# One decoder block on one core: output projection by pairs of tiles, merged gate broadcasts, dense queries as float32r passes, constants filled in another place

## Chip, core and metric

One core of one Trainium2 chip. The metric is device microseconds from start to end of one execution; lower is better. The kernel before was timed three times.

## What is computed

One layer of a hybrid decoder block on 512 tokens of width 1024 (float32), cut from the reference:

```python
def rmsnorm(x, w):
    return x * rsqrt(mean(x * x, -1) + eps) * w

h = rmsnorm(x, norm_mix_w)                      # 1. mixer
proj = h @ w_in                                  # gated-DeltaNet group (4 heads) | mLSTM group (4 heads)
go = gated_delta_rule(...)                       # chunkwise recurrences with per-token gates
mh = mlstm_chunkwise(...)
x = x + concatenate([go, mh], -1) @ w_out        # output projection

q = rmsnorm(x, norm_xa_w) @ xa_wq                # 2. cross-attention to 256 memory tokens
k, v = split(rmsnorm(mem, norm_mem_w) @ xa_wkv, 2)
x = x + (softmax(q k^T / 16) v) @ xa_wo

# 3. PEER: per token and head, top-16 of 2 x 128 product keys -> 16 of 16384 experts, then gather
sc = einsum('thpd,hpnd->thpn', rmsnorm(x, norm_ffn_w) @ peer_wq, sub_keys)
x = x + sum_k gate_k * gelu(u[expert_k] . h) * v[expert_k]
```

## The kernel before

The 512 tokens are four tiles of 128. A matmul that must keep float32's accuracy is done in one of two ways. **Split:** `weights` loads a 512 KB piece into a buffer `w` (a DMA on SP's queue, line 246), ACT copies it to float32r (`hi`, line 236, or line 251 into other buffers), DVE or POOL subtracts that from the raw piece (`low`: line 223 on DVE, line 221 on POOL; the list `low_on` says whose turn it is), and three matmul passes hi·hi, hi·lo, lo·hi follow (line 271 in `proj`, line 284 in `projT`). **Whole:** the piece is used as float32 (line 313 in `times`), with no copy. The activations are split in the same manner when they are transposed (`transposed`: PE line 209, ACT line 211, DVE line 212), or kept whole (`whole`: lines 293 and 294).

The mixer (0 to 445 us) projects head by head, and runs the two recurrences' chains under the projections; a string, `ORDER_MIX`, sets the order in which the program writes these steps, and the tile framework's scheduler then orders each engine's instructions. Each head takes from `gates` the rows `br` (three kinds: the GDN's cumulated decay, and two for mLSTM) and broadcasts them over the partitions with a matmul against a selector `sel`: one per token tile into a quarter of a PSUM bank for a GDN head (line 452, read by DVE lines 454 and 455 and ACT line 456), one of 256 columns per tile into a bank for an mLSTM head (line 564, read by DVE line 566 and ACT line 568). The pool of those banks (`psB`, name `acc`) has two buffers.

The mixer's output projection is `residual`, called with all four tiles and `wout`: `proj` goes over two blocks of 512 columns, over four 512 KB pieces each, and over the four tiles, so that a piece serves 24 matmuls. `residual`'s evacuation adds the result to `X` (DVE line 699). Buffers `w`, `wh` and `wl` are two each.

Then `ORDER_XA` gives the program's order, with tiles 0 and 1 as the pair G0 (experts gathered row by row) and tiles 2 and 3 as the dense pair G1: `n` is the norm of a pair (ACT line 197 squares, DVE lines 174 to 183 the reciprocal root, DVE line 199 scales by the row `wr`), `q` its queries (`q104` means G1's blocks 0 to 3, `q148` its blocks 4 to 7), `s` and `x` the attention, `o` its output projection, `i0` the norm and transposes of G0 for the expert layer, `f0` and following that layer's scores. G0's queries are split (line 284), G1's are whole (line 313). The row `wr` is loaded on SP's queue into a weight buffer `wh`. POOL fills `rows_` (constants of the routing) with 48 small memsets at lines 1148 to 1150, behind the mixer.

Of the kernel before, what the change touches and what calls it, by code (L numbers as in the profile page):

```python
# [16 lines left out]
P = 128  # L17
# [38 lines left out]
ORDER_XA = ("w2 n0 q008 n1 s0 x0 s1 x1 q104 o0 w1 i0 q148 f0 f1 r6 "  # L56
# [19 lines left out]
def _body(ctx, tc, A, out, dbg):  # L76
# [248 lines left out]
    def bank4():  # L325
        return psB.tile([P, 4, P], F32, name="acc")
# [36 lines left out]
    def gates(ph, wk, hs, tiles):  # L363
# [58 lines left out]
        for i in range(n):  # L422
# [8 lines left out]
        return {ti: dict(beta=beta[:, i], cum=cum[:, i], enm=enm[:, i], br=br[:, i], cj=cj[:, i], beg=beg[:, i])  # L431
                for i, ti in enumerate(tiles)}

    def gdn(wk, items, gs, qkv, mixed):
# [15 lines left out]
        bc = bank4()  # L450
        for i, (h, ti) in enumerate(items):
            PE.matmul(bc[:, i], sel[:, h], gs[ti]["br"][:, 0], start=True, stop=True)
# [102 lines left out]
    def mlstm(wk, items, gs, qk, va, mixed):  # L555
# [5 lines left out]
        ET, es = wt("ET", 2), wt("eg", 2)  # L561
        for i, (h, ti) in enumerate(items):
            bc = bank()
            PE.matmul(bc[:, :256], sel[:, h], gs[ti]["br"][:, 1:3].rearrange("p a b -> p (a b)"),
                      start=True, stop=True)
            V.scalar_tensor_tensor(ET[:, i], bc[:, 128:256], gs[ti]["cj"][:, h:h + 1], maskT,
                                   op0=OP.add, op1=OP.add)
            SC.activation(es[:, i], bc[:, 0:128], AF.Exp)
# [30 lines left out]
    def mixer(tiles, aside):  # L599
        nt = len(tiles)  # L600
        with tc.tile_pool(name="mxp", bufs=nt) as ph, tc.tile_pool(name="mxw", bufs=2) as wk:
# [89 lines left out]
            residual(tiles, hs, "wout")  # L691
# [11 lines left out]
    def xattn():  # L703
# [4 lines left out]
        wr = row(1, wpool, name="wh")  # L708
# [18 lines left out]
        def query(g, blocks):  # L727
            def ev(nb, ps):
                SC.activation(qT[:, nb, cols(g)], ps, AF.Copy)
            if "f" in part(g):  # L730
                projected(part(g)["f"], len(g), A["wq"], blocks, ev)
            else:
                projT(part(g), len(g), A["wq"], blocks, ev)
# [401 lines left out]
    t = late.tile([P, 2, DB, 2 * P], F32R, name="dh0")  # L1135
    dh.append({"h": t[:, 0], "l": t[:, 1]})
    t = late.tile([P, 4, D], F32, name="dh1")
    dh.append({"f": eight(t), "room": t})
# [8 lines left out]
    for a in range(K):  # L1147
        G.memset(rows_[:, 0, a], float(start[a]))
        G.memset(rows_[:, 1, a], float(start[a] - start[a - 1] if a else 0))
        G.memset(rows_[:, 2, a], float(a))  # L1150
# [46 lines left out]
    for what in ORDER_XA.split():  # L1197
# [3 lines left out]
        elif kind == "q":  # L1201
            n, x, y = (int(c) for c in what[1:])
            query(GS[n], range(x, y))
        elif kind == "s":
# [26 lines left out]
        elif kind == "f":  # L1231
            first.scores(n)
# [93 lines left out]
```

## Time and profile before

| | |
|---|---|
| median of 3 runs | 1864.69 us (1860.12 to 1868.1) |
| the profiled execution | 1863.43 us |
| its span, first to last instruction | 1861.5 us |
| PE busy in the span | 1682.0 us (90%) |
| DVE busy | 1248.2 us (67%) |
| POOL busy | 849.9 us (46%) |
| ACT busy | 393.9 us (21%) |
| DMA traffic | 514.81 MB |

Times are microseconds unless marked ns. PE is the matmul engine, PEld its weight loads, DVE the vector engine, ACT the scalar engine, POOL GpSimd, SP the queue on which most transfers are issued. A name such as `pj<-W,dh` is output from inputs, by the program's names; L271 is line 271. Idle time in brackets stands ahead of the instruction, with what ended it. Matmuls overlap: their pitch is read from the distance of two starts, not from one's duration.

### The profile page before, as it was taken

What the parts mean: (1) busy time and instruction counts of PE and PEld (TensorE: products, weight loads), DVE (VectorE), ACT (ScalarE), POOL (GpSimd) and SP (SyncE); (2) the same over time, 40 slices, a digit from 0 to 9 for tenths busy, and PEclk for the clock granted to TensorE, in tenths of its full rate; (3) what the DMA queues carried; (4) which work ended last, traced back from release to release, by engine and by line L of the source; (5) the groups of instructions that cost most, each with busy time, mean ns of one, the idle gap of its engine ahead of it and who ended that gap; (6) DMA issues with size and microseconds to landing.
All of it is one profiled execution on the core that took longest, in us unless ns stands there. A gap on an engine that the chain in (4) does not pass through costs nothing.

```text
span 1861.5 us, 21345 instructions
## 1 busy us (share of the span) xinstructions
PE 1682.0 (90%) x7444; PEld 1240.6 (67%) x7444; DVE 1248.2 (67%) x2767; ACT 393.9 (21%) x784; POOL 849.9 (46%) x686
## 2 busy tenths in 40 slices
PE   4999999999799986996998979993899999999993
PEld 3787777787698863885887746662666666664441
DVE  5656655473422598999998876557666566566668
ACT  5433442564243121111222210000000000000000
POOL 2121111323312044567344656666666666666663
PEclk9999999999899988998999979997999999999997
DMA  4111111234524477999799999999999999999996
GB/s 138 63 57 35 57 40 46 69 102 149 168 88 162 149 261 269 350 335 372 259 332 408 367 385 410 410 410 410 410 410 410 409 410 409 410 409 409 409 411 257
DMA packets 165355, 514.81 MB, mean 277 GB/s; under 512 B 15616, under 2 KB 44416, under 8 KB 163456
## 3 DMA queue, kind: packets, MB, share of 16 engines
q0 software_dynamic: 76608, 286.30, 39.3%
q1 hardware_dynamic: 59712, 212.48, 30.9%
q10 hardware_dynamic: 28928, 14.68, 2.7%
q8 instruction: 58, 0.95, 0.2%
q14 instruction: 49, 0.40, 0.1%
HBM read 494.52 MB, written 18.87 MB: 276 GB/s over the span
## 4 chain that ended last, share of the span: by engine, by line
DMA 38%; PE 33%; DVE 19%; issue 4%; POOL 3%; ACT 2%; SPq 0%; DVEq 0%; POOLq 0%; ACTq 0%
PE pj L313 7%; PE pj L271 7%; DMA row<-in_pv,ids 7%; PE pj L284 6%; DMA W<-in_pv,ids 6%; DMA Vm<-in_pv,ids 5%; PE acc L445 4%; DMA row<-in_pu,ids 3%; DMA wl<-in_pv,ids 3%; DMA W<-gates__132 3%; PE acc L945 2%; DMA gates__132<-W 2%; DVE W L1100 2%; DMA wl<-in_pu,ids 2%; DMA KT<-in_pv,ids 1%
## 5 line engine op out<-in xcount | busy, mean ns | idle before, releaser
L1000 PE MATMUL o<-ld,W 128*128 128x512 f32 x832 | 370.9, 596 | 4.6 <-DVE W L953 4.6
L313 PE MATMUL pa<-dh,ld 128*128 128x256 f32 x1296 | 295.5, 381 | 34.7 <-ACT dh L972 34.2
L313 PEld LDWEIGHTS pa<-dh,ld 128*128 128x128 f32 x1296 | 247.3, 191 | 103.1 <-issue 38.2
L1000 PEld LDWEIGHTS o<-ld,W 128*128 128x128 f32 x832 | 158.8, 191 | 175.7 <-issue 167.3
L221 POOL TENSOR_TENSOR wl<-w,wh 128x1024 fp32r<-128x1024 f32 x38 | 92.4, 2434 | 348.8 <-ACT wh L236 294.7
L313 PE MATMUL pj<-dh,w 128*128 128x256 f32 x704 | 161.3, 383 | 0.0
L313 PEld LDWEIGHTS pj<-dh,w 128*128 128x128 f32 x704 | 133.4, 193 | 17.8 <-ACT dh L294 0.3
L1073 POOL DMA_INDIRECT W<-in_pu,ids x73 | 95.4, 1307 | 91.0 <-DVE W L1100 52.2
L1111 DVE SCALAR_TENSOR_TENSOR dh<-row,act,dh 128x1024 f32<-128x1024 f32 x72 | 92.5, 1284 | 53.8 <-DMA row<-in_pv,ids 53.5
L1073 POOL DMA_INDIRECT row<-in_pu,ids x74 | 98.5, 1331 | 64.4 <-issue 17.8
L1073 POOL DMA_INDIRECT row<-in_pv,ids x74 | 99.9, 1351 | 47.2 <-issue 17.9
L313 PE MATMUL pj<-dh 128*128 128x256 f32 x496 | 113.2, 383 | 0.0
L284 PE MATMUL pj<-hT,wh 128*128 128x512 f32 x320 | 111.9, 421 | 0.0
L972 ACT ACTIVATE W<-pa 128x256 f32<-128x256 f32 x65 | 25.0, 384 | 407.2 <-PE pa L313 397.5
L271 PE MATMUL pj<-wh,hT 128*128 128x512 f32 x320 | 106.1, 404 | 0.4 <-ACT hT L211 0.4
L1100 DVE SCALAR_TENSOR_TENSOR row<-row,dh 128x1024 f32<-128x1024 f32 x74 | 88.3, 1223 | 22.4 <-DMA row<-in_pu,ids 22.1
L313 PEld LDWEIGHTS pj<-dh 128*128 128x128 f32 x496 | 94.5, 193 | 12.6
L1100 DVE SCALAR_TENSOR_TENSOR W<-W,dh 128x1024 f32<-128x1024 f32 x73 | 88.4, 1221 | 17.2 <-DMA W<-in_pu,ids 17.2
L236 ACT ACTIVATE wh<-w 128x1024 fp32r<-128x1024 f32 x56 | 59.3, 1059 | 124.2 <-PE pj L271 64.1
L1000 PE MATMUL o<-ld,dh 128*128 128x512 f32 x192 | 85.2, 592 | 0.0
L1073 POOL DMA_INDIRECT wl<-in_pu,ids x41 | 56.6, 1380 | 49.1 <-DVE tv L783 18.6
L1073 POOL DMA_INDIRECT wh<-in_pu,ids x40 | 54.2, 1354 | 49.9 <-DVE wh L1100 22.3
(431 smaller groups left out, 3106.5 us busy)
## 6 DMA issues: line engine op xcount, KB each, us to landing
ld<-in_pv SPq DMA_DIRECT2D x128, 512.0 KB, 6.8
ld<-in_pt SPq DMA_DIRECT2D x81, 512.0 KB, 6.9
gates__132<-W ACTq DMA_DIRECT2D x16, 896.0 KB, 13.9
W<-gates__132 POOLq DMA_DIRECT2D x14, 1024.0 KB, 17.1
w<-in_pt SPq DMA_DIRECT2D x24, 512.0 KB, 6.9
dh<-in_pt SPq DMA_DIRECT2D x23, 512.0 KB, 6.9
w<-in_win SPq DMA_DIRECT2D x20, 512.0 KB, 3.5
w<-in_pwq SPq DMA_DIRECT2D x16, 512.0 KB, 4.7
```

The source lines that it names most:

```text
L221: G.tensor_tensor(out, a, hi, op=OP.subtract)
L236: SC.activation(hi, wt, AF.Copy)
L271: PE.matmul(acc[i], a[:, d, i * P:(i + 1) * P], b[:, z], start=d == 0 and m == 0, stop=d == DB - 1 and m == len(pairs) - 1)
L284: PE.matmul(acc[:, :n * P], a[:, d], b[:, d], start=d == 0 and m == 0, stop=d == DB - 1 and m == 2)
L313: PE.matmul(ps, w[:, d], h[:, d], start=d == 0, stop=d == DB - 1)
L445: PE.matmul(ps[:, i], l[:, i], r[:, i], start=True, stop=True)
L945: PE.matmul(ps[:, k], oj[:, a, :, k], og[:, g, a, :, k], start=g == 0, stop=g == 1)
L972: SC.activation(place(e), ps, AF.Gelu)
L1000: PE.matmul(outs[DENSE[i]][z], place(e)[:, i * P:(i + 1) * P], v[:, z * 512:(z + 1) * 512], start=e == 0, stop=e == NKEY - 1)
L1073: G.indirect_dma_start(out=row, out_offset=None, in_=A[table], in_offset=bass.IndirectOffsetOnAxis(ap=ids[:, s:s + 1], axis=0))
L1100: V.scalar_tensor_tensor(row, row, 1.0, hn, op0=OP.mult, op1=OP.mult, accum_out=act[ti][:, s:s + 1])
L1111: V.scalar_tensor_tensor(hn, row, w, hn, op0=OP.mult, op1=OP.add)
```

## The change

- **Output projection:** `low_on` becomes DVE alone, and `residual` is called twice, for tiles 0 and 1 and then for tiles 2 and 3, each with the whole of `wout`.
- **Broadcasts:** a GDN head broadcasts its decay row for all four tiles with one matmul of 512 columns, and an mLSTM head its two rows with two of 512 columns into two banks; ACT's exponential of the second is one instruction for four tiles.
- **Dense queries:** `query` uses the split path for both pairs, so that `norm` and `mix` write G1's transposes split too; the buffer `dh1` becomes float32r and is opened again as float32 after `q148`. `q148` moves ahead of `i0`.
- **Row `wr`:** loaded on POOL's queue into the last sixth of a big buffer (`up[:, 5]`), not on SP's into `wh`.
- **Constants:** `rows_` is filled by the same 48 memsets just ahead of the first scores (`f0`).

```diff
-ORDER_XA = ("w2 n0 q008 n1 s0 x0 s1 x1 q104 o0 w1 i0 q148 f0 f1 r6 "
+ORDER_XA = ("w2 n0 q008 n1 s0 x0 s1 x1 q104 o0 w1 q148 i0 f0 f1 r6 "
...
         bc = bank4()
+        PE.matmul(bc[:, :n], sel[:, items[0][0]], gs["br"][:, :, 0], start=True, stop=True)
         for i, (h, ti) in enumerate(items):
-            PE.matmul(bc[:, i], sel[:, h], gs[ti]["br"][:, 0], start=True, stop=True)
...
+        bc = [bank4(), bank4()]
+        for x in (1, 0):
+            PE.matmul(bc[x][:, :n], sel[:, items[0][0]], gs["br"][:, :, 1 + x], start=True, stop=True)
         for i, (h, ti) in enumerate(items):
-            bc = bank()
-            PE.matmul(bc[:, :256], sel[:, h], gs[ti]["br"][:, 1:3].rearrange("p a b -> p (a b)"),
-                      start=True, stop=True)
-            V.scalar_tensor_tensor(ET[:, i], bc[:, 128:256], gs[ti]["cj"][:, h:h + 1], maskT,
-                                   op0=OP.add, op1=OP.add)
-            SC.activation(es[:, i], bc[:, 0:128], AF.Exp)
+            V.scalar_tensor_tensor(ET[:, i], bc[1][:, i], gs[ti]["cj"][:, h:h + 1], maskT, op0=OP.add, op1=OP.add)
+        SC.activation(es, bc[0][:, :n], AF.Exp)
...
-            residual(tiles, hs, "wout")
+            low_on[:] = [V]
+            for k in range(0, nt, 2):
+                residual(tiles[k:k + 2], {z: t[:, :, k * P:(k + 2) * P] for z, t in hs.items()}, "wout")
...
-        wr = row(1, wpool, name="wh")
+        wr = row_(1, up[:, 5], G)
...
-            if "f" in part(g):
-                projected(part(g)["f"], len(g), A["wq"], blocks, ev)
-            else:
-                projT(part(g), len(g), A["wq"], blocks, ev)
+            projT(part(g), len(g), A["wq"], blocks, ev)
...
-    t = late.tile([P, 2, DB, 2 * P], F32R, name="dh0")
-    dh.append({"h": t[:, 0], "l": t[:, 1]})
-    t = late.tile([P, 4, D], F32, name="dh1")
-    dh.append({"f": eight(t), "room": t})
+    for i in range(2):
+        t = late.tile([P, 2, DB, 2 * P], F32R, name=f"dh{i}")
+        dh.append({"h": t[:, 0], "l": t[:, 1]})
...
-    for a in range(K):
-        G.memset(rows_[:, 0, a], float(start[a]))
-        G.memset(rows_[:, 1, a], float(start[a] - start[a - 1] if a else 0))
-        G.memset(rows_[:, 2, a], float(a))
+
+    def row_numbers():
+        for a in range(K):
+            for x, val in enumerate((start[a], start[a] - start[a - 1] if a else 0, a)):
+                tc.keep_in_program_order(G.memset(rows_[:, x, a], float(val)))
...
             query(GS[n], range(x, y))
+            if n and y == DB:
+                t = late.tile([P, 4, D], F32, name="dh1")
+                dh[1] = {"f": eight(t), "room": t}
...
+            if not n:
+                row_numbers()
             first.scores(n)
```

ACT's order at the end of the output projection (`wh` the float32r copy of a piece of `wout`, the L197 rows the squares of the first pair's norm, L251 the copies of the first query weights; the brackets name the engines and queues waited for). Before:

```order
L236 ACTIVATE wh<-w 128x1024 [waits DMAHW4_49,PE_49,Pool_49]
L236 ACTIVATE wh<-w 128x1024 [waits DMAHW5_49,DVE_49,PE_49]
L197 ACTIVATE W_4106,nss<-x 128x1024 [waits DMAHW7_49,DVE_49,PE_49]
L197 ACTIVATE W_4106,nss<-x 128x1024 [waits DVE_49]
L251 ACTIVATE W_4105<-w 128x1024 [waits DMAHW6_49]
L251 ACTIVATE W_4105<-w 128x1024 [waits DMAHW7_49]
```

and now:

```order
L236 ACTIVATE wh<-w 128x1024 [waits DMAHW3_49,DVE_49,PE_49]
L236 ACTIVATE wh<-w 128x1024 [waits DMAHW4_49,DVE_49,PE_49]
L236 ACTIVATE wh<-w 128x1024 [waits DMAHW5_49,DVE_49,PE_49]
L197 ACTIVATE W_4066,nss<-x 128x1024 [waits PE_49]
L197 ACTIVATE W_4066,nss<-x 128x1024
L251 ACTIVATE W_4065<-w 128x1024 [waits DMAHW6_49]
L251 ACTIVATE W_4065<-w 128x1024 [waits DMAHW7_49]
```

The squares still stand behind the last copy of `wout` and still wait for PE; no copy waits for POOL any more.

DVE's order through the output projection to the start of the norm (L223 the lows, L212 the activations' lows, L699 or L700 the evacuations, L174 the norm's first step). Before:

```order
L223 TENSOR_TENSOR wl<-w,wh 128x1024 x2
L212 TENSOR_TENSOR hT<-tr,hT 128x4x128 x8
L223 TENSOR_TENSOR wl<-w,wh 128x1024
L699 TENSOR_TENSOR x<-pj,x 128x512 x4
L223 TENSOR_TENSOR wl<-w,wh 128x1024
L699 TENSOR_TENSOR x<-pj,x 128x512 x4
L174 TENSOR_SCALAR nv<-nss 128x1
```

and now, from the first evacuation on:

```order
L700 TENSOR_TENSOR x<-pj,x 128x512
L223 TENSOR_TENSOR wl<-w,wh 128x1024
L700 TENSOR_TENSOR x<-pj,x 128x512
L223 TENSOR_TENSOR wl<-w,wh 128x1024 x3
L700 TENSOR_TENSOR x<-pj,x 128x512
L223 TENSOR_TENSOR wl<-w,wh 128x1024
L700 TENSOR_TENSOR x<-pj,x 128x512
L223 TENSOR_TENSOR wl<-w,wh 128x1024 x3
L700 TENSOR_TENSOR x<-pj,x 128x512 x2
L174 TENSOR_SCALAR nv<-nss 128x1
```

All lows of `wout` are DVE's, between the evacuations of each pair; the norm's first step still follows the last evacuations.

PE's order from the attention's output projection (L271 with 512 columns, 96 matmuls) to the expert layer's scores (L313 from `dh_4764` before, from `dh_4916` now), with the dense pair's queries (L313 from `dh_4049` before, L284 now) and the first pair's transposes (L293). Before:

```order
L271 MATMUL pj<-W_4105,dh_4048 128x512 x96
L313 MATMUL pj<-dh_4049,w 128x256 x11
L293 MATMUL tr<-UI,dh_4764 128x128 x8
L313 MATMUL pj<-dh_4049,w 128x256 x2
L293 MATMUL tr<-UI,dh_4764 128x128 x8
L313 MATMUL pj<-dh_4049,w 128x256 x3
L313 MATMUL pj<-dh_4049,W_4106 128x256 x16
L313 MATMUL pj<-dh_4764,w 128x256 x16
```

and now:

```order
L284 MATMUL pj<-dh_4057,W_4065 128x256 x68
L271 MATMUL pj<-W_4065,dh_4056 128x512 x96
L284 MATMUL pj<-dh_4057,W_4065 128x256 x96
L293 MATMUL tr<-UI,dh_4916 128x128 x16
L313 MATMUL pj<-dh_4916,w 128x256 x16
```

The last four query blocks are 96 split matmuls in a row now, and all 16 transposes stand behind them, ahead of the scores.

## Rows read from the trace of the kernel before

**Rows 1.** The page: its part 4, the chain of work that ended last, by engine.
```profile
DMA 38%; PE 33%; DVE 19%; issue 4%; POOL 3%; ACT 2%; SPq 0%; DVEq 0%; POOLq 0%; ACTq 0%
```

**Rows 2.** Busy time of each engine by stage (windows of the span; a row has the window, its length, then PE, PEld, DVE, ACT and POOL busy with their instruction counts, the granted TensorE clock as a share of full speed, the DMA engines' busy share and GB/s).
```profile
36.00:424.00 388.00, 370.87 (x2122) 303.27 (x2121) 230.69 (x574) 173.38 (x337) 80.98 (x37) 0.97 0.19 60
...
445.50:493.40 47.90, 47.61 (x215) 38.15 (x216) 12.67 (x17) 11.40 (x15) 12.72 (x6) 1.00 0.44 153
493.40:508.60 15.20, 4.17 (x19) 3.19 (x17) 13.14 (x35) 7.85 (x12) 6.95 (x50) 0.60 0.68 216
...
532.30:566.10 33.80, 33.80 (x179) 28.45 (x178) 7.23 (x13) 17.52 (x42) 2.35 (x1) 1.00 0.26 79
...
588.20:604.80 16.60, 15.94 (x82) 13.65 (x81) 6.25 (x27) 5.51 (x11) 0.00 (x0) 1.00 0.45 159
...
655.00:1100.00 445.00, 384.87 (x1917) 317.81 (x1916) 411.64 (x1251) 95.58 (x198) 239.34 (x196) 0.93 0.92 333
1100.00:1830.00 730.00, 695.72 (x2237) 425.88 (x2235) 465.58 (x464) 30.04 (x79) 471.71 (x358) 0.98 1.02 409
```

**Rows 3.** Timeline of the end of the memory's value projection (`wv`), which works on two tiles with the same weight path: start, duration, engine, line, operation, and in brackets the engine's idle time before it and what ended that.
```profile
435.50 1.06 ACT L236 ACTIVATE wh<-w 128x1024 fp32r<-128x1024 f32 x1 [3.71 <-DMA w<-in_wv]
...
439.04 1.64 SPq L246 DMA_DIRECT2D w<-in_wout  x2
...
439.06 0.50 PE L271 MATMUL pj<-wl,x 128*128 128x512 f32 x1 [1.44 <-POOL wl L221]
439.09 1.23 DVE L223 TENSOR_TENSOR wl<-w,wh 128x1024 fp32r<-128x1024 f32 x1 [7.34 <-ACT wh L236]
...
442.73 1.06 ACT L236 ACTIVATE wh<-w 128x1024 fp32r<-128x1024 f32 x1 [3.67 <-DMA w<-in_wout]
```

**Rows 4.** DMA issues between 380 and 500 us (count, size of one, median us from issue to landing), and the last line of the view of line 246, which issues the split weights' loads, between 400 and 560 us.
```profile
w<-in_wout SPq DMA_DIRECT2D x8, 512.0 KB, 3.7
x<-in_x SPq DMA_DIRECT2D x1, 2048.0 KB, 7.6
...
DMA to landing us min/median/max: 3.4/3.6/7.0
```

**Rows 5.** Timeline of the output projection's last two matmuls.
```profile
493.18 0.40 PE L271 MATMUL pj<-wl,hT 128*128 128x512 f32 x1
...
493.41 0.40 PE L271 MATMUL pj<-wh,hT 128*128 128x512 f32 x1
```

**Rows 6.** Timeline from the output projection's end to the first query matmul.
```profile
497.06 2.35 POOL L221 TENSOR_TENSOR W<-w,W 128x1024 fp32r<-128x1024 f32 x1 [0.89 <-ACT W L251]
...
499.37 2.34 POOL L221 TENSOR_TENSOR W<-wl,W 128x1024 fp32r<-128x1024 f32 x1
...
499.46 3.33 DVE L199 SCALAR_TENSOR_TENSOR W<-x,nr,wh 128x1024 f32<-128x1024 f32 x1
...
502.89 1.94 PE L209 MATMUL tr<-UI,W 128*128 128x128 f32 x8 [9.08 <-issue]
...
505.36 1.28 DVE L199 SCALAR_TENSOR_TENSOR W<-x,nr,wh 128x1024 f32<-128x1024 f32 x1
...
508.56 12.62 PE L284 MATMUL pj<-dh,W 128*128 128x256 f32 x97
```

**Rows 7.** The norm row's load in the timeline; the DMA issues of that row's kind between 480 and 515 us (size, median us to landing); then, from the view of line 191 (all loads of rows in the kernel: duration of the issue in ns, first and last start), an issue on POOL and the times to landing.
```profile
488.39 0.42 SPq L191 DMA_DIRECT2D wh<-in_nrow  x1
...
wh<-in_nrow SPq DMA_DIRECT2D x2, 512.0 KB, 5.4
...
L191 POOL DMA_DIRECT2D Vm<-in_nrow x1: 555/555/555, 1707.4 to 1707.4; - x1
...
DMA to landing us min/median/max: 5.4/7.9/17.4
```

**Rows 8.** Timeline of the queries: two evacuations of split query blocks on ACT (six blocks lie between the two rows), then the end of the dense pair's queries with the first pair's transposes for the expert layer, on PE, to the first matmul of that layer's scores.
```profile
516.35 0.36 ACT L729 ACTIVATE W<-pj 128x256 f32<-128x256 f32 x1
...
532.61 0.39 ACT L729 ACTIVATE W<-pj 128x256 f32<-128x256 f32 x1 [2.50 <-PE pj L284]
...
588.17 4.91 PE L313 MATMUL pj<-dh,w 128*128 128x256 f32 x22
593.30 1.06 PE L293 MATMUL tr<-UI,dh 128*128 128x128 f32 x8 [0.23 <-DVE nt L181]
...
595.66 1.06 PE L293 MATMUL tr<-UI,dh 128*128 128x128 f32 x8 [0.43 <-DVE dh L199]
...
597.86 7.07 PE L313 MATMUL pj<-dh,W 128*128 128x256 f32 x32
604.77 1.46 PE L313 MATMUL pj<-dh,w 128*128 128x256 f32 x6
```

**Rows 9.** The gates' broadcasts of the last mLSTM head in the timeline (a row merges the two broadcasts of 256 columns; each matmul leaves two records), what PE waited for at the broadcasts up to 446 us (total, times, longest), and one window of 25 us.
```profile
410.27 1.13 PE L564 MATMUL acc<-br,sel 4*128 4x256 f32 x4
...
412.95 1.12 PE L564 MATMUL acc<-br,sel 4*128 4x256 f32 x4 [0.67 <-ACT eg L568]
...
PE acc L452 <- DVE EG L455: 1.2, 1, 1.2
...
PE acc L564 <- ACT eg L568: 0.7, 1, 0.7
...
125.00:150.00 25.00, 24.49 (x94) 18.61 (x93) 13.13 (x36) 10.62 (x18) 2.41 (x1) 0.80 0.19 64
```

More of the change, by code (lines that the diff above doesn't have):

```diff
@@ L430, in gates @@
         V.tensor_tensor(beg, beg, beta, op=OP.mult)
-        return {ti: dict(beta=beta[:, i], cum=cum[:, i], enm=enm[:, i], br=br[:, i], cj=cj[:, i], beg=beg[:, i])
-                for i, ti in enumerate(tiles)}
+        return {"br": br, **{ti: dict(beta=beta[:, i], cum=cum[:, i], enm=enm[:, i], cj=cj[:, i], beg=beg[:, i])
+                             for i, ti in enumerate(tiles)}}
     def gdn(wk, items, gs, qkv, mixed):
```

## The prediction

> **What bounds the kernel now.** I read the chain of waits first: DMA holds 38% of it, PE 33%, DVE 19% [rows 1]. No one engine bounds the whole, so the next view is the one by stages [rows 2]. From 1100 to 1830 us the DMA engines are busy all the time at 409 GB/s, from 655 to 1100 us DVE is busy for 411.64 of 445 us with DMA at 0.92: these are the gathers and the dense experts, and the change doesn't touch them. Ahead of them PE is full: 370.87 of 388 us in the mixer's main part, 47.61 of 47.9 us in the output projection, all of 33.8 us at the attention, 15.94 of 16.6 us at the last dense queries. One stage is different: from 493.4 to 508.6 us PE works for 4.17 us, and the granted clock is 0.60 in the mean, so in part at the lower of its two levels (1.2, not 2.4 GHz). That is the norm between the projection and the queries.
>
> From the first scores of the expert layer (604.77 us, [rows 8]) the instruction order of every engine is the same before and after the change. So the result is the shift of that one moment, carried to the end; nothing behind it has slack to swallow a few microseconds, as the DMA stage is full. I sum up the shift, part by part, against the profiled execution (1863.43 us, of which the span is 1861.5). It lies 1.3 us below the median of the three runs.
>
> **Output projection by pairs: +3.7 us.** The matmuls are the same 192, at a pitch of 0.23 us [rows 5]. But a piece of `wout` now serves 12 of them, 12 x 0.2325 = 2.79 us, and so is loaded twice: 16 loads, 16 ACT copies, 16 lows on DVE, where there were 8 each. Does the supply keep up? The value projection ahead of it has just that shape, two tiles and 12 matmuls a piece, and PE waited there [rows 3]: 1.44 us for a low on POOL, while ACT had been idle 3.71 and 3.67 us for the load. One buffer's round is the load, from the issue at 439.04 to the copy at 442.73, 3.7 us, plus the copy, 1.06, plus a low on DVE, 1.23 [rows 3], with some 0.06 of handing over: 6.07 us. With two buffers that is 3.03 us a piece against 2.79, so 0.24 x 16 = 3.9 us at most. A replay of the rounds by hand, with `x` (2 MB, 7.6 us, [rows 4]) ahead of the third load and a start that hides the first two pieces, moves the projection's end from 493.8 to 497.5. Lower bound 0: the transposes at the start spread the first four pieces, and every load might land in the minimum of 3.4 us [rows 4], which gives 2.88 us a piece. Upper bound +9.4: in the value projection two pieces took 442.73 - 435.50 = 7.23 us [rows 3], 3.6 a piece, which would be 0.82 x 16 = 13 us less what the start hides. I take 3.7, since POOL's 2.4 us lows, part of those 3.6, are gone.
>
> **The gap behind it: 0.** It would be the obvious gain of pairs that the first pair's norm lies under the second pair's matmuls. The order says otherwise: ACT's squares stand behind the 14 last copies and wait for PE, DVE's chain stands behind the last evacuations. What follows is as before: squares, chain, and then the place where POOL's lows (497.06 to 501.71 us) hold DVE [rows 6]: the scaling of the first tile takes 3.33 us, that of the second, without POOL, 1.28. Both lows of the query weights stay on POOL, so PE again gets its first transpose some 9 us after the end, and its first query some 14.8 us after it (508.56 - 493.8).
>
> The row `wr` is the other question there. Before it was issued at 488.39, ahead of the projection's end [rows 7]. Now POOL issues it, and the memory that it goes to is set free only with the last matmul. An issue on POOL takes 0.56 us, landing 5.4 at the least, 7.9 in the median, 17.4 at the most [rows 7]. It is needed when DVE comes free of POOL's lows, 501.71 - 493.8 = 7.9 us after the end [rows 6]. So it costs 0 at 0.56 + 5.4 = 6.0, 0.6 at the median and 10.1 at the worst. I take 0, as the two such loads of this stage have 5.4 for their median [rows 7].
>
> **Merged broadcasts: -3 us.** PE streams as many columns as before; 12 matmul issues and handovers a head fall away, and in the mLSTM heads 12 exponentials of ACT become fewer and longer ones. Where does that reach the path? In the last head the second pair of broadcasts started 412.95 - 410.27 = 2.7 us behind the first, as the banks had to be read by DVE and ACT [rows 9]. Behind it the chain runs over the head's norm on DVE to the low that frees the buffer for `wout` (439.04, [rows 3]), so nearly all of it counts. Of the earlier heads' waits little does: PE itself waited for a broadcast's readers only 1.2 and 0.7 us in the whole mixer [rows 9]. I take 2.7 plus a little of these: 3. Bounds: a loss of 2, since one matmul of 512 columns must now wait for a whole bank, and since lows and chains change places on DVE; a gain of 7, of the 388 - 370.87 = 17.1 us in which PE is idle in this stage [rows 2].
>
> **Dense queries split: -2.4 and -3.25 us.** A whole block of 256 tokens-by-columns takes 7.07 / 2 = 3.5 us (3.45 between evacuations); a split one takes (532.61 - 516.35) / 6 = 2.71 us, though it has three passes [rows 8]. For the four blocks in the attention's stage, where PE is full [rows 2], that is 4 x 0.74 = 2.9 us less; I take off 0.5 for ACT's copy (1.06) in front of the attention's own evacuations, so -2.4, with -3 and -1 as ends. The other four now stand before `i0`. From 588.17 to 604.77, 16.6 us, PE did four whole blocks, 16 transposes (two rows of 1.06 us) and 0.66 us of waiting [rows 8]. After: 4 x 2.71 = 10.84, and 16 transposes behind it with their evacuations, 2.5 us, 13.35 in all: -3.25. The norm of G0 is hidden by these blocks: before, both tiles' transposes were ready by 595.66, 7.5 us from the stage's start, and 10.84 us cover that. The lows and copies of eight more pieces lie beside PE's work on ACT (17.52 of 33.8 us busy) and DVE (7.23) [rows 2]; were that cover gone, PE would wait a low of POOL, 2.35 us, a piece.
>
> **Constants: 0.** POOL's 48 memsets end before the low at 497.06, which waited 0.89 us for ACT [rows 6]. At the new place POOL has no one waiting for it.
>
> **Sum:** 3.7 + 0 - 3 - 2.4 - 3.25 = -4.95 us, 1858.5 by the profiled execution and 1859 to 1860 by the median; I say 1859. A measurement of this kernel can tell about 0.5%, 9.3 us, from no change; so the limits are 1855.4 and 1874.
>
> **The rivals.**
> First, the mixer gains more. Between 125 and 150 us the granted clock is 0.80 [rows 9]: that is 10 us at the lower level, 5 us of full work. If the merged GDN broadcasts take away the wait that lies ahead of it, another 7 us go (5, and the 1.2 + 0.7 of waits): 1852. For it: the broadcast heads each GDN chain. Against: the long waits of PE there come from the chain itself, not from line 452.
> Second, the change does what pairs seem to offer, and the first norm hides under the second pair: then PE's 9.08 us of idle time go, 1850. The order speaks against it.
> Third, the slower side: the loads set the projection's pace. From 3.03 us a piece on each further tenth costs 1.6 us; at the value projection's 3.6 us the projection costs 13, not 3.7: 1868, over the median before, and 1871 or more where the broadcasts give nothing. For it: the trace had loads of up to 7.0 us [rows 4], and `x` lies among these. Against: POOL is out of the round.
> Fourth, the row lands late, and DVE waits up to 10.1 us for it, with PE behind: 1869. For it: it now starts with the gap. Against: 5.4 us in this stage.
> A rule of the Trainium skill speaks against this move of the row: in SBUF — State Buffer, section on the two separate sides, its warning on DVE blocking a DMA says that descriptors of a DMA from GpSimd's queue can't be written while DVE runs an operation in a two-port mode. No run here shows it; by that rule the issue would wait for what DVE then runs, the last evacuation or a 128x1 step, and the sum would be worse by under 1 us.
>
> **How the numbers follow.** Forecast 62%, own range 1852 to 1867; first rival 14%, second 5%, third 13%, fourth 6%. Faster than 1855.4: 8 of the forecast's 62, with 13 of the first rival and 5 of the second, 26%. Slower than 1874: 4 of the third and 1 of the fourth, 5%. The rest, 69%, is within 0.5%. The range 1849 to 1870 leaves out some 2 in 10: the ends of the first two rivals below, of the last two above.
>
> **What would show it.** In the profile after: 16 copies of `wout` on ACT at a spacing near 3.0 us, with PE waiting for DVE's lows, and an end of the projection less than 4 us later in its own stage; the gap again near 15 us, with DVE's scaling held by POOL; no wait for the row; the last mLSTM broadcasts less than 1 us apart; query blocks at 2.7 us; and the first scores at about 599.7 us instead of 604.77. I am wrong if that moment moves by a different amount, or if it moves so and the end doesn't follow.

## The result and the profile after

The changed kernel took 1853.3 us in the median (1851.97 to 1853.88, 4 runs) against 1865.51 for the kernel before (1860.12 to 1868.1, now 4 runs): a ratio of 0.9922, 95% interval 0.9895 to 0.9949 (the two medians alone stand at 0.9935). It is faster, by 0.7 to 0.8%. Medians here and below are of runs at the usual mean clock (0.95 to 0.96 granted); one of the ten runs of the kernel with four broadcasts in a row took 2454.67 us at 0.65 and is left out. The forecast was 1859 within 1849 to 1870; the time is in the range, and past the limit of 1855.4 for "faster by over 0.5%", which had 26%. The span of the profiled run went from 1861.5 to 1851.6 us, 9.9 less.

The stages by landmarks, starts read from the two timelines (the first matmul of the projection, its last matmul's end, the first query matmul, the first matmul of the scores):

| | before | after | shift | forecast |
|---|---|---|---|---|
| mixer, to the first projection matmul | 445.56 | 434.25 | -11.3 | -3 |
| output projection | 48.25 | 53.17 | +4.9 | +3.7 |
| gap, to the first query | 14.75 | 15.12 | +0.4 | 0 |
| queries and attention, to the first scores | 96.21 | 91.72 | -4.5 | -5.65 |
| from there to the end | 1256.7 | 1257.3 | +0.6 | 0 |
| sum | | | -9.9 | -4.95 |

So one term is far off, the mixer's, and the others are near. The chain and the stages of the changed kernel, beside [rows 1] and [rows 2]:

```profile
DMA 36%; PE 33%; DVE 17%; issue 8%; POOL 4%; ACT 2%; ACTq 1%; SPq 0%; DVEq 0%; POOLq 0%
```

```profile
0.00:434.20 434.20, 395.19 (x2225) 320.31 (x2226) 260.42 (x707) 196.21 (x366) 95.75 (x57) 0.98 0.23 72
434.20:487.30 53.10, 49.74 (x215) 36.87 (x213) 27.41 (x30) 19.80 (x23) 0.00 (x0) 1.00 0.60 198
487.30:502.50 15.20, 3.82 (x17) 3.14 (x16) 13.20 (x34) 7.85 (x12) 5.38 (x3) 0.63 0.77 275
...
524.40:558.00 33.60, 33.60 (x228) 30.41 (x227) 12.24 (x19) 20.15 (x46) 5.04 (x3) 1.00 0.32 99
...
580.10:594.30 14.20, 13.75 (x114) 13.19 (x112) 8.44 (x29) 7.28 (x14) 4.64 (x49) 1.00 0.71 240
```

The windows have the columns of [rows 2]. The mixer's window, which starts at 0 here, is 434.2 long and PE is busy for 395.19 of it. PE is idle for 39.0 us; in the kernel before, the same stretch of 445.5 us had 403.9 busy and 41.6 idle:

```profile
0.00:445.50 445.50, 403.85 (x2262) 326.79 (x2262) 262.26 (x705) 199.31 (x380) 98.52 (x58) 0.98 0.22 71
```

Most of the gain, 8.7 of 11.3 us, is thus busy time of PE, although PE streams the same columns. The projection is no longer full: 49.74 of 53.1 us, where it was 47.61 of 47.9. The gap is as before, and the queries' stages are shorter, with PE busy for 33.60 of 33.6 and 13.75 of 14.2 us.

The projection in the timeline, ACT's copies of `wout` first, then what ACT waited for in the stage (total, times, longest), beside [rows 3]:

```profile
445.24 1.06 ACT L236 ACTIVATE wh<-w 128x1024 fp32r<-128x1024 f32 x1 [1.55 <-DMA w<-in_wout]
448.95 1.06 ACT L236 ACTIVATE wh<-w 128x1024 fp32r<-128x1024 f32 x1 [2.65 <-DMA w<-in_wout]
451.54 1.06 ACT L236 ACTIVATE wh<-w 128x1024 fp32r<-128x1024 f32 x1 [1.53 <-DMA w<-in_wout]
454.90 1.06 ACT L236 ACTIVATE wh<-w 128x1024 fp32r<-128x1024 f32 x1 [2.30 <-DMA w<-in_wout]
```

```profile
ACT wh L236 <- DMA w<-in_wout: 24.3, 12, 2.8
```

Three pieces take 454.90 - 445.24 = 9.66 us, 3.2 each; 3.03 was worked out. ACT waits for loads 12 times, 24.3 us in all.

The gap, beside [rows 6]:

```profile
487.74 0.74 POOL L191 DMA_DIRECT2D W<-in_nrow  x1 [59.46 <-PE pj L271]
...
490.68 2.34 POOL L221 TENSOR_TENSOR W<-w,W 128x1024 fp32r<-128x1024 f32 x1 [2.21 <-ACT W L251]
...
492.99 2.33 POOL L221 TENSOR_TENSOR W<-wl,W 128x1024 fp32r<-128x1024 f32 x1
...
493.14 2.20 DVE L181 TENSOR_TENSOR nt<-nr 128x1 f32<-128x1 f32 x1
...
495.82 1.28 DVE L199 SCALAR_TENSOR_TENSOR W<-x,nr,W 128x1024 f32<-128x1024 f32 x1 [0.28 <-DMA W<-in_nrow]
...
497.20 1.94 PE L209 MATMUL tr<-UI,W 128*128 128x128 f32 x8 [9.78 <-issue]
...
498.80 1.28 DVE L199 SCALAR_TENSOR_TENSOR W<-x,nr,W 128x1024 f32<-128x1024 f32 x1
...
502.54 12.66 PE L284 MATMUL pj<-dh,W 128*128 128x256 f32 x94
```

POOL's two lows (490.68 to 495.32) hold DVE until 495.3 again, this time not in the scaling but in steps of 128x1: two steps of L183 that start at 490.76 take 2.35 us together, one of L181 at 493.14 takes 2.20, where its like take 0.15 to 0.16. The row, issued by POOL at 487.74, landed at about 495.8, and DVE waited 0.28 us for it.

The end of the dense queries and the transposes, beside [rows 8]:

```profile
580.12 11.68 PE L284 MATMUL pj<-dh,W 128*128 128x256 f32 x96
591.63 1.04 PE L293 MATMUL tr<-UI,dh 128*128 128x128 f32 x8
592.92 1.14 PE L293 MATMUL tr<-UI,dh 128*128 128x128 f32 x8 [0.25 <-ACT dh L294]
594.26 7.17 PE L313 MATMUL pj<-dh,w 128*128 128x256 f32 x32 [0.20 <-ACT dh L294]
```

Four split blocks took 591.63 - 580.12 = 11.5 us, 2.88 each, and the transposes 2.6.

The broadcasts, beside [rows 9]: one GDN head in the changed kernel, and the same window of 25 us.

```profile
61.99 0.40 PE L284 MATMUL pj<-hT,wl 128*128 128x512 f32 x1
62.32 1.12 PE L451 MATMUL acc<-br,sel 4*128 4x512 f32 x2
63.37 1.05 PE L464 MATMUL acc<-ones,Zm 128*128 128x1 f32 x8
...
125.00:150.00 25.00, 24.57 (x105) 19.01 (x103) 14.91 (x43) 12.27 (x22) 2.68 (x2) 0.86 0.22 64
```

One broadcast of 512 columns takes PE from 62.22, where the next float32r matmul would have come (61.99 + 0.23), to 63.37: 1.15 us for four tiles. What follows there is float32 too (`L464`).

### The profile page after: what moved, and what is told of

The parts are those of the page before. It is cut to its first block, busy times and chain, and to the rows that moved or that the text cites. A ratio compares the mean times of both kernels' runs of the same rounds, so it can differ in the third digit from the quotient of the medians.

```text
span 1851.6 us, 21460 instructions
## 1 busy us (share of the span) xinstructions
PE 1671.7 (90%) x7468; PEld 1233.1 (67%) x7468; DVE 1269.1 (69%) x2789; ACT 406.2 (22%) x786; POOL 842.2 (45%) x685
## 4 chain that ended last, share of the span: by engine, by line
DMA 36%; PE 33%; DVE 17%; issue 8%; POOL 4%; ACT 2%; ACTq 1%; SPq 0%; DVEq 0%; POOLq 0%
DMA row<-in_pv,ids 8%; PE pj L313 8%; PE pj L284 7%; PE pj L271 5%; PE acc L445 4%; DMA wh<-in_pv,ids 4%; DMA Vm<-in_pv,ids 3%; DMA W<-gates__132 3%; PE acc L943 3%; DMA W<-in_pv,ids 3%; DMA row<-in_pu,ids 3%; DMA wl<-in_pv,ids 2%; DVE W L1098 2%; DMA wl<-in_pu,ids 2%; DMA KT<-in_pu,ids 2%
## 5 line engine op out<-in xcount | busy, mean ns | idle before, releaser
L313 PE MATMUL pa<-dh,ld 128*128 128x256 f32 x1296 | 295.7, 381 | 35.8 <-ACT dh L970 34.2
L313 PEld LDWEIGHTS pa<-dh,ld 128*128 128x128 f32 x1296 | 247.4, 191 | 104.1 <-issue 39.3
L221 POOL TENSOR_TENSOR wl<-w,wh 128x1024 fp32r<-128x1024 f32 x32 | 76.9, 2408 | 307.6 <-ACT wh L236 265.8
L313 PE MATMUL pj<-dh,w 128*128 128x256 f32 x640 | 148.0, 387 | 0.2 <-ACT dh L294 0.2
L313 PEld LDWEIGHTS pj<-dh,w 128*128 128x128 f32 x640 | 122.6, 195 | 17.2 <-ACT dh L294 0.7
L970 ACT ACTIVATE W<-pa 128x256 f32<-128x256 f32 x65 | 24.9, 383 | 407.6 <-PE pa L313 397.5
L313 PE MATMUL pj<-dh 128*128 128x256 f32 x496 | 111.7, 379 | 0.0
L271 PE MATMUL pj<-wh,hT 128*128 128x512 f32 x320 | 108.5, 410 | 1.3 <-ACT wh L236 1.3
L284 PE MATMUL pj<-hT,wh 128*128 128x512 f32 x320 | 109.1, 414 | 0.0
L313 PEld LDWEIGHTS pj<-dh 128*128 128x128 f32 x496 | 93.5, 191 | 12.2
L236 ACT ACTIVATE wh<-w 128x1024 fp32r<-128x1024 f32 x64 | 67.7, 1058 | 106.8 <-DMA w<-in_wout 27.7
```

What stands on the lines that cost most here:

```text
L221: G.tensor_tensor(out, a, hi, op=OP.subtract)
L236: SC.activation(hi, wt, AF.Copy)
L271: PE.matmul(acc[i], a[:, d, i * P:(i + 1) * P], b[:, z], start=d == 0 and m == 0, stop=d == DB - 1 and m == len(pairs) - 1)
L284: PE.matmul(acc[:, :n * P], a[:, d], b[:, d], start=d == 0 and m == 0, stop=d == DB - 1 and m == 2)
L313: PE.matmul(ps, w[:, d], h[:, d], start=d == 0, stop=d == DB - 1)
L970: SC.activation(place(e), ps, AF.Gelu)
```

## The experiments

All times are medians, the ratio is that to the kernel before run on the same chip, with its 95% interval. The edits are shown against the changed kernel, but for the first.

**Broadcasts alone** (kernel before, with the change's two hunks on the broadcasts and the one on `gates`' result):

```diff
         bc = bank4()
+        PE.matmul(bc[:, :n], sel[:, items[0][0]], gs["br"][:, :, 0], start=True, stop=True)
         for i, (h, ti) in enumerate(items):
-            PE.matmul(bc[:, i], sel[:, h], gs[ti]["br"][:, 0], start=True, stop=True)
...
+        bc = [bank4(), bank4()]
+        for x in (1, 0):
+            PE.matmul(bc[x][:, :n], sel[:, items[0][0]], gs["br"][:, :, 1 + x], start=True, stop=True)
...
```

> The kernel before with the merged broadcasts alone. The mixer's part of the shift in the profile after was -11.3 us (first projection matmul 445.56 to 434.25) where 3 were forecast. Theory, switches: a float32 broadcast of 128 columns between float32r matmuls takes some 0.62 us of PE's time there (65.80 + 0.23 to the next regular pitch), of which its columns are 0.21; merging four of them saves 1.2 us a GDN head, and 0.4 an mLSTM head, 6 us, and waits go with it: 7 to 11 us faster than before, some 1855 to 1858. Rival, as the prediction had it: only the last head's chain counts, 3 us, 1862. Rival, the mixer's gain comes from something else of the change (the memory of the row, the constants, DVE's lows at its end): 1865, as before.

1851.3 us, ratio 0.9934 (0.9909 to 0.9958). The projection's first matmul came at 433.37 us, as in the changed kernel (434.25). So the broadcasts bring the mixer's whole gain, and within the intervals as much as the whole change; its other parts about cancel. The median is below the 1855 to 1858 us that were expected. The profiled run was this kernel's slowest (1859.95 us): from the first matmul of the product keys (`L822`) to the end it took 1250.5 us, where the kernel before took 1242.9 and the changed one 1243.4. Why that part was longer in this one profile is open; the mixer lies ahead of it.

**Projection whole:**

```diff
-            low_on[:] = [V]
-            for k in range(0, nt, 2):
-                residual(tiles[k:k + 2], {z: t[:, :, k * P:(k + 2) * P] for z, t in hs.items()}, "wout")
+            residual(tiles, hs, "wout")
```

> The changed kernel with the output projection for all four tiles in one call again, its lows on DVE and POOL in turn. Theory: pairs cost what the trace shows, a projection of 53.1 us instead of 48.3, so this is 4.8 us faster than the changed kernel, 1848.5. Rival: the pairs' loads were hidden by something that now comes late elsewhere (query weights loaded earlier, accumulators freed earlier), and the time stays at 1853. Rival: pairs were what made the mixer's end earlier, and it is slower, 1857 or more.

1845.4 us, ratio 0.9906 (0.988 to 0.9932): the projection took 48.2 us, the gap 14.75, and the pairs' 5 us were gone. Neither rival holds. Its interval overlaps the changed kernel's, so it is the trace that tells the two apart.

**Dense queries whole again:**

```diff
-ORDER_XA = ("w2 n0 q008 n1 s0 x0 s1 x1 q104 o0 w1 q148 i0 f0 f1 r6 "
+ORDER_XA = ("w2 n0 q008 n1 s0 x0 s1 x1 q104 o0 w1 i0 q148 f0 f1 r6 "
...
-            projT(part(g), len(g), A["wq"], blocks, ev)
+            if "f" in part(g):
+                projected(part(g)["f"], len(g), A["wq"], blocks, ev)
+            else:
+                projT(part(g), len(g), A["wq"], blocks, ev)
...
```

> The changed kernel with the dense pair's queries whole in float32 again, the transposes with them, and the order i0 q148 as before. Theory: the queries' stages took 91.7 us instead of 96.2 from the first query to the first scores, so this is 4.5 us slower than the changed kernel, 1858. Rival: the prediction's full 5.65 us, 1859. Rival: nothing, since the stage behind takes it back, 1853.

1857.4 us, ratio 0.9964 (0.9943 to 0.9986). The queries' share shows in the trace: from the first query to the first matmul of the product keys it took 110.9 us; the kernel before had 110.0, the changed one 105.6. That is 4.4 to 5.3 us, near the 4.5 of the theory. Over all profiles it is 110.0 to 111.2 us with these queries whole and 105.3 to 107.6 with them split.

**GDN broadcasts apart:**

```diff
-        PE.matmul(bc[:, :n], sel[:, items[0][0]], gs["br"][:, :, 0], start=True, stop=True)
         for i, (h, ti) in enumerate(items):
+            PE.matmul(bc[:, i], sel[:, h], gs[ti]["br1"][:, 0], start=True, stop=True)
```

> The changed kernel with the four broadcasts of each GDN head apart again; mLSTM's stay merged. Theory, switches: 4 heads at 1.2 us and about 1 of waits, 5 to 6 us slower than the changed kernel, 1858 to 1859. Rival, only the last mLSTM head's chain counts: no change, 1853. Rival, the half-clock stretch between 132 and 148 us hangs on these broadcasts: then its 0.83, 0.50, 0.50, 0.89 come back as they were before, where the changed kernel has 0.54 and 0.60 in 8 us, and the time is 1855.

1861.2 us, ratio 0.9982 (0.9953 to 1.001), and the projection began at 449.15. The interval lies above the changed kernel's (0.9895 to 0.9949) and overlaps that of its repeat (0.9913 to 0.9963, below). Of the 14.9 us by which the projection begins later than in the changed kernel, 8.5 go to the clock (17.1 us lost in the mixer instead of 8.6): as the second rival had it, the half-clock stretch came back, and longer (a granted clock of 0.73, 0.50, 0.50 and 0.50 in the four windows from 132 to 148 us, where the changed kernel has 1.00, 0.54, 0.60 and 1.00). What is left without the clock is some 6 us (the table below). One of the four broadcasts of a head, on PE:

```profile
64.74 0.40 PE L271 MATMUL pj<-wl,hT 128*128 128x512 f32 x1
65.07 0.48 PE L452 MATMUL acc<-br,sel 4*128 4x128 f32 x2
65.48 0.74 PE L271 MATMUL pj<-wh,hT 128*128 128x512 f32 x2
66.06 0.40 PE L271 MATMUL pj<-wl,hT 128*128 128x512 f32 x1
```

Behind the float32r matmul at 64.74 the next would come at 64.97. The broadcast starts at 65.07, the next float32r matmul at 65.48, and the two that start there last till 66.06, where two pitches would end at 65.95. So a broadcast of 128 columns takes 0.51 us until float32r goes on, 0.62 with what is lost behind it; four of them, each alone, would be 2.5. The merged one, of the same columns, takes 1.15 until PE goes on, though there with float32. PE's record shows all of this as busy.

**Four in a row** (the number of matmuls of the last run, with the neighbours of the changed kernel):

```diff
-        PE.matmul(bc[:, :n], sel[:, items[0][0]], gs["br"][:, :, 0], start=True, stop=True)
+        for i, (h, ti) in enumerate(items):
+            tc.keep_in_program_order(PE.matmul(bc[:, i], sel[:, h], gs["br"][:, ti, 0], start=True, stop=True))
```

> The changed kernel with each GDN head's broadcast in four matmuls of 128 columns again, but issued one right behind the other, ahead of all that read them. PE's number of matmuls is that of the run with the GDN broadcasts apart, the number of changes between float32r and float32 that of the changed kernel. Theory, changes between the two: as the changed kernel, first projection matmul at 434 to 435 us, time the same within 0.1%. Rival, each matmul and its handing over costs: as the run with them apart, 6 us of PE's time more at the full clock, 440 us and later.

1850.8 us, ratio 0.9935 (0.991 to 0.996); the projection began at 428.16. On PE:

```profile
60.87 0.40 PE L284 MATMUL pj<-hT,wl 128*128 128x512 f32 x1
61.19 1.15 PE L452 MATMUL acc<-br,sel 4*128 4x128 f32 x8
62.27 1.05 PE L465 MATMUL acc<-ones,Zm 128*128 128x1 f32 x8
```

Four matmuls in one go take from 61.10 to 62.27, 1.17 us, as the merged one does. A later head compares the three kernels with float32r right behind the broadcast. In the changed kernel:

```profile
195.67 0.39 PE L530 MATMUL acc<-S,cv 128*128 128x128 f32 x2
195.99 1.12 PE L451 MATMUL acc<-br,sel 4*128 4x512 f32 x2
197.04 0.50 PE L284 MATMUL pj<-hT,wh 128*128 128x512 f32 x1
```

The merged broadcast takes 1.05 us from its start to float32r (195.99 to 197.04), four in a row 1.08 (189.79 to 190.87), and with them apart it is 0.41 for the first, which also stands behind `L530` (200.29 to 200.70), and 0.62 for each of three lone ones (at 201.84, 203.62 and 205.40): 2.27 us. So it isn't the number of matmuls that costs, it is each lone float32 matmul between float32r ones.

**The changed kernel again**, as the measure for that hour:

> The changed kernel itself once more, on the chip and in the hour of the next three, as their measure. Its ratio to the kernel before was 0.992; single runs of one kernel scatter by some 0.5% on either side here, so 0.989 to 0.996 is expected, and the first projection matmul near 434 us.

1853.9 us, ratio 0.9938 (0.9913 to 0.9963), the projection at 429.52.

**mLSTM broadcasts apart:**

```diff
-        bc = [bank4(), bank4()]
-        for x in (1, 0):
-            PE.matmul(bc[x][:, :n], sel[:, items[0][0]], gs["br"][:, :, 1 + x], start=True, stop=True)
         for i, (h, ti) in enumerate(items):
+            bc = bank()
+            PE.matmul(bc[:, :256], sel[:, h], gs[ti]["br1"][:, 1:3].rearrange("p a b -> p (a b)"),
+                      start=True, stop=True)
```

> The changed kernel with the mLSTM heads' broadcasts apart again, GDN's merged. From the first head's first matmul to the first projection matmul, less what the clock lost, the kernel before took 397.5 us, GDN alone apart 395.2, all merged 387.6 to 390.1. Theory, changes between float32r and float32 (some 7 of the 17 that are saved): 2 to 3.5 us more than the changed kernel, 391 to 393, of which the last head's chain would be up to 2.7. Rival: none of it counts, 388 to 390.

1854.8 us, ratio 0.995 (0.9931 to 0.9969). The stretch less the clock's share is 390.8, at the upper end of the merged kernels' 387.6 to 390.8: by one profile the mLSTM heads' merging is worth 0 to 3 us, no more can be said.

**Four buffers for the pieces of `wout`:**

```diff
             low_on[:] = [V]
+            raws.extend(wk.tile([P, 3, NT, P], F32, name="cv").rearrange("p x a b -> p (x a b)")[:, :D] for _ in range(2))
+            raws.extend(wpool.tile([P, 2, 512], F32, name="w").rearrange("p a b -> p (a b)") for _ in range(2))
             for k in range(0, nt, 2):
```

> The changed kernel, projection by pairs, but the raw pieces of wout go through four buffers (two lie in a buffer of the GDN heads that is free by then) where there were two; hi and lo keep two each. Theory, the supply sets the pace: a round of 6 us over four buffers is 1.5 us a piece, so the pairs' matmuls (2.79) set it again, the projection takes 48.3 to 49.5 us instead of 53 to 56, and the time comes to that of the whole projection. Rival, DVE's lows or the copies set the pace: the projection stays at 53 us or over.

1844.2 us, ratio 0.9893 (0.9859 to 0.9927). The projection by pairs took 47.4 us now. ACT's copies, and its waits in the stage:

```profile
437.44 1.06 ACT L236 ACTIVATE wh<-cv 128x1024 fp32r<-128x1024 f32 x1 [1.72 <-PE pj L271]
440.24 1.06 ACT L236 ACTIVATE wh<-cv 128x1024 fp32r<-128x1024 f32 x1 [1.74 <-PE pj L271]
443.04 1.06 ACT L236 ACTIVATE wh<-w 128x1024 fp32r<-128x1024 f32 x1 [1.74 <-PE pj L271]
```

```profile
ACT wh L236 <- PE pj L271: 21.6, 13, 1.7
```

They stand 2.80 us apart, the pairs' matmuls, and ACT waits for PE where it waited for loads. So the supply through two buffers was the whole cost of pairs.

**The row on SP:**

```diff
-        wr = row_(1, up[:, 5], G)
+        wr = row(1, wpool, name="wh")
```

> The changed kernel with the norm's row loaded by SP into the weight buffer again. In the profile after, DVE's scaling waited 0.28 us for the row, at 495.82, 8.4 us after the projection's end. Theory: nothing else hangs on it, so 0 to 0.5 us faster, not to be told apart in the time, and the 0.28 us wait is gone. Rival, the row's place mattered: the weight buffer that it takes is one that the projection's loads need at the end, and the projection gets longer by a round of 3 us.

1852.0 us, ratio 0.9922 (0.9898 to 0.9946), not to be told from the changed kernel. The gap was 14.7 us. The projection took 56.2 us here, but kernels with the row on POOL took 53.2 to 55.8 as well, so the rival is not excluded, and not shown.

**Projection whole, row on SP, no lows on POOL in the gap:**

```diff
-            low_on[:] = [V]
...
+            residual(tiles, hs, "wout")
...
-        wr = row_(1, up[:, 5], G)
+        wr = row(1, wpool, name="wh")
...
-    low_on[:] = [V, G]
+    low_on[:] = [V]
...
             query(GS[n], range(x, y))
+            low_on[:] = [V, G]
```

> The output projection whole, as in the second run, the row on SP as before, and all lows of the first pair's queries on DVE, so that POOL runs none in the gap behind the projection. Theory: in the gap (14.8 us) DVE is held by two of POOL's lows, 497.06 to 501.71 before; its chain ends some 3.4 us after the projection, then the scaling, 1.28, instead of 3.3 that start late; the first transposes come some 5 us after the end instead of 9.1, the gap shrinks to 10 to 11 us, and the time is 4 us under the second run's. Rival: DVE's own lows (1.23 each) and the row's landing take the place of POOL's, and the gap stays at 14 to 15 us.

1845.8 us, ratio 0.9898 (0.9868 to 0.9928). The first half of the theory held: the projection ended at 479.55, DVE's scaling of the first tile (483.08) took 1.28 us, 3.5 us after the end, and PE's first transposes came 4.9 us after the end. The second half fell:

```profile
483.08 1.28 DVE L199 SCALAR_TENSOR_TENSOR W<-x,nr,wh 128x1024 f32<-128x1024 f32 x1
...
484.35 1.22 DVE L223 TENSOR_TENSOR W<-w,W 128x1024 fp32r<-128x1024 f32 x1
...
484.46 1.59 PE L209 MATMUL tr<-UI,W 128*128 128x128 f32 x8 [4.91 <-issue]
...
485.56 1.22 DVE L223 TENSOR_TENSOR W<-w,W 128x1024 fp32r<-128x1024 f32 x1
...
487.95 1.22 DVE L223 TENSOR_TENSOR W<-wl,W 128x1024 fp32r<-128x1024 f32 x1
...
489.67 1.28 DVE L199 SCALAR_TENSOR_TENSOR W<-x,nr,wh 128x1024 f32<-128x1024 f32 x1
...
491.10 1.94 PE L209 MATMUL tr<-UI,W 128*128 128x128 f32 x8 [5.04 <-DVE nt L181]
492.87 0.58 PE L284 MATMUL pj<-dh,W 128*128 128x256 f32 x1
```

Three lows on DVE now lie ahead of the second tile's scaling (489.67), PE waits 5.04 us more for it, and the gap is 13.3 us, not 10 to 11. With the projection whole and the row on SP but POOL's lows kept (the next run) it is 14.7, so the lows' place is worth 1.4. From the first query to the product keys it then took 107.6 us (105.3 to 106.6 in the other profiles with split queries), so of the 1.4 us little stays.

**Whole, row on SP:** the two edits together.

> The best of both: merged broadcasts and split dense queries of the changed kernel, projection whole and the row on SP as before. From the runs so far: 0.990 to 0.991 of the kernel before; the projection at 48.3 us, the gap at 14.7.

1843.3 us, ratio 0.9883 (0.9852 to 0.9914): the shortest time, with the run on four buffers beside it (0.9893). Its interval overlaps that of the changed kernel (0.9895 to 0.9949) at its upper end, and only touches that of the repeat (0.9913 to 0.9963).

The mixer in all profiles: the time from the first head's first matmul to the projection's first, then what the clock lost in it (each window of 4 us up to 440, its length times the share by which the granted clock fell short of 1), and the difference (its median over the ten profiles of the last row is 389.1); behind it how often PE changes there from float32r (lines 271, 284 and 371) to a stretch of float32 matmuls, counted in the trace:

| broadcasts | us | clock | difference | stretches |
|---|---|---|---|---|
| before, both apart | 407.7 | 10.2 | 397.5 | 142 |
| GDN apart | 412.3 | 17.1 | 395.2 | 136 |
| mLSTM apart | 395.9 | 5.1 | 390.8 | 132 |
| merged (changed kernel twice, seven others) or four in a row | 390.8 to 397.8 | 0 to 8.6 | 387.6 to 390.8 | 126 |

## Why the prediction was right or wrong

The time fell in the range, but the sum didn't come out: by the prediction's own sign the first scores were to move from 604.77 to about 599.7 us, and another shift was to mean that it is wrong. They moved to 594.26, 10.5 us instead of 5. One term was 8.3 us too small, and the others together 3.35 us too favourable, which hid part of it. That the time is in the range owes something to luck and to the range's width of 21 us.

**Merged broadcasts, -3: mis-sized; measured -11.3 in the profile.** The step that failed is the sentence that PE streams as many columns as before, from which only the last head's chain was counted. The columns are the same, but a float32 matmul that stands alone between float32r matmuls takes some 0.3 to 0.4 us beyond its columns (0.51 to 0.62 us, where two records of 128 columns, 0.11 us apart inside the row of four, make 0.21 to 0.22), and the change removes 16 such places of 142. The experiments show it: with the broadcasts alone the projection starts as early as in the whole change; with GDN's apart the difference in the table is 6.1 us over the merged kernels' median, 0.6 for each of ten stretches more; with four in a row, the same matmuls without the neighbours, it is 388.0, as merged. The price per place explains 3 to 4 of those 6.1 us, and a wait of PE at one broadcast (1.2 us, at `L452`, also in that run) another part; the rest is within the 3.2 us by which the merged profiles differ among themselves, and is not shown. The forecast's "12 matmul issues a head" is wrong too: a GDN head has three matmuls fewer and an mLSTM head two, 20 in all.

The table's difference accounts for 8.3 of the 11.3 us. The rest: the first head's matmuls began 1.4 us earlier in this profile, and the clock lost 8.6 instead of 10.2 us. Both scatter between profiles of kernels with merged broadcasts (start 34.7 to 36.5, clock 0 to 8.6), and the kernel before has one profile, so how much of them belongs to the change is open.

The rows for this lay in the trace of before, where a lone `L452` row takes 0.6 us of PE's time out of the pitch of its neighbours:

```profile
65.80 0.40 PE L271 MATMUL pj<-wl,hT 128*128 128x512 f32 x1
66.13 0.48 PE L452 MATMUL acc<-br,sel 4*128 4x128 f32 x2
66.54 0.74 PE L271 MATMUL pj<-wh,hT 128*128 128x512 f32 x2
67.12 0.40 PE L271 MATMUL pj<-wl,hT 128*128 128x512 f32 x1
```

At a pitch of 0.23 us the three float32r starts behind 65.80 would take 0.70 us; the third comes 1.32 us behind it. I read the pitch within a row of merged records, and not the pitch across it.

**The first rival** gave 1852, near the time. Its mechanism is at most a small part here: the half-clock stretch between 125 and 150 us didn't go, the granted clock there is 0.86 instead of 0.80, and PE lost 8.6 us to the clock in the mixer instead of 10.2. But over all profiles that clock is 0.86 to 1.00 in the eleven with GDN's broadcasts merged or in a row, and 0.80 and 0.68 in the two with them apart. So the rival may hold in part; two profiles don't settle it. Waits of PE at the broadcasts (1.2 and 0.7 us) are gone, and others came (1.2 us at `L590`, 0.9 at `L445`).

**The last head's chain**, the one thing that was counted, is at most a part: with the mLSTM heads apart the difference is 390.8, 0 to 3 us more than merged. No run tells the chain from the changes between the two types there.

**Pairs, +3.7: right in mechanism, somewhat small.** 4.9 us in the profile, 4.8 to 8.0 by all profiles (53.2 to 56.2 us by pairs with two buffers, 48.2 to 48.4 whole). The round through two buffers was worked out at 3.03 us a piece and measured at 3.2. The four buffers show the cause: with more of them the cost is gone, and the pairs even beat the whole projection by 0.8 us. The third rival, 3.6 us a piece, was too much; that the low on POOL, which is out of the round, makes the difference is likely but wasn't tried.

**The gap, 0: right.** 15.12 against 14.75 us. The second rival, the first norm under the second pair, didn't occur, as the order of instructions said. That POOL's lows hold DVE is now shown: without them DVE's first scaling is over 4.8 us after the projection's end (483.08 + 1.28 - 479.55), with them it was 9.0 us in the kernel before. But my reading that the gap hangs on it was too simple, since DVE's own lows take their place in front of the second tile.

**The row: right within 0.3 us.** It landed 8.0 us after its issue, the median of 7.9 rather than the 5.4 that I took; DVE waited 0.28 us. The fourth rival, 10 us, didn't occur.

**Dense queries, -2.4 and -3.25: right in mechanism, too large by a fifth.** 4.5 us instead of 5.65. The term that was mis-sized is the 2.71 us a block. It was the mean between two evacuations on ACT, [rows 8], and the first of these came late, behind a copy (515.38 to 516.44 us); the last ones, at 526.85, 529.73 and 532.61, stand 2.88 us apart, which is PE's own pitch. Eight blocks at 0.17 us are 1.4 us, a little more than the 1.15 that are missing (0.4 in the attention's stage, 0.8 behind it).

**Constants, 0:** nothing contradicts it; it wasn't tried alone.

That the shift of the first scores is carried to the end held within 0.6 us in this pair of profiles: 10.5 us there, 9.9 at the end. In general it holds less well: from the first matmul of the product keys to the end the thirteen profiles took 1241.4 to 1250.5 us.

## What to carry to other kernels

Where two element types of matmul share the matmul engine, count the changes between them in its order of instructions, not only the columns: here a lone float32 matmul among float32r ones cost as much as two to three times its columns, and gathering four of them, merged or one behind the other, gave more than any other part of the change. A matmul engine that is busy all the time can still hold such losses, and they are read from the pitch of the neighbours, start to start, not from the busy share. When a stage is cut so that a piece of the weights serves fewer matmuls, compare the round of one buffer (load, copy, low), divided by the buffers, with the matmuls that it feeds; a third and fourth raw buffer gave back all of the 5 us here.

## What the runs showed of the hardware that I had not expected

- A change from float32r to a single float32 matmul and back took 0.3 to 0.4 us of PE's time beyond the columns, mostly recorded as busy: 64.97 to 65.48 us for 128 columns, whereas 512 columns took 1.15 us and four times 128 in a row 1.17, and 1.05 and 1.08 where float32r follows.
- The granted clock falls to the lower of its two levels (1.2 GHz) for stretches of up to some 17 us in the mixer, and not at the same places in profiles of the same instructions: the changed kernel lost 8.6 us to it once and 6.8 us the next time, first at 64 to 72 us in the one and at 36 to 44 in the other, and the run with four buffers lost none. In the window of 4 us ahead of the fall behind 64 us PE is recorded as busy for 4.00 us; in the other profile the clock falls within the window from 36 to 40 us (0.88 granted), in which PE is busy for 2.74 us. The kernels with GDN's broadcasts apart lost 10.2 and 17.1 us, those with them merged 0 to 8.6; whether the lone matmuls cause that is not settled.
- Steps of DVE on 128x1 elements are held by a low on POOL as a big one is: one took 2.20 us (493.14), where its like take 0.15 to 0.16.
- POOL's issue of the row took 0.74 us, where another such issue took 0.56 [rows 7], and the row landed 8.0 us behind it. The Trainium skill (SBUF — State Buffer, the section on the two separate sides) says that a DMA from GpSimd's queue can't get its descriptors written while DVE runs an operation in a two-port mode. No run here shows a wait of that kind: the run with the row on SP brings no gain that the time could tell.
